# Eight instead of sixteen pairs of expert tiles in fixed order, four of them last; scatters at an even pace in the text; first gates, then places

## The chip, the core and the metric

The kernel runs on one core of a Trainium2 chip. The metric is the time of one execution on the device, in microseconds, the median of several runs. The engines are named as in the profile: PE is TensorE (matmuls), DVE VectorE, ACT ScalarE, POOL GpSimd, SP SyncE, which issues most of the transfers.

## The reference, cut to what matters

Two transformer blocks are computed for 256 tokens of width 1024. The change is in the last layer, a lookup among 16384 experts: every token picks 16 experts in each of eight heads, and only their values count.

```python
def _peer(h, w_q, subkeys, w_down, w_up):
    ...
        tv, tj = lax.top_k(cand, PEER_TOPK)
        eidx = jnp.take_along_axis(cidx, tj, axis=-1)
        w = jax.nn.softmax(tv, axis=-1)
        u = w_down[eidx]
        a = jax.nn.gelu(jnp.einsum('btd,btpkd->btpk', hblk, u).astype(jnp.float32))
        vv = w_up[eidx]
        return jnp.einsum('btpk,btpkd->btd', (w * a).astype(hblk.dtype), vv)
...
        x = x + ga2[:, None, :] * _peer(h, w_peer_q[l], peer_subkeys[l], peer_down[l], peer_up[l])
    return _rms_norm(x, g_norm_final)
```

## The kernel before

The kernel goes the other way round: it multiplies all tokens with all experts, and multiplies the result by a matrix of gates G that is zero where a token did not pick an expert. The 16384 experts are 128 tiles of 128, taken in 64 pairs, e = 0 to 63. The 256 tokens are two halves, tt = 0 and 1.

**Down.** `more_down` loads the down rows of one pair (`wr<-dn`), splits them into a high and a low part (`wh` on ScalarE, `wl` on VectorE), makes 48 matmuls of 256 columns and applies gelu; the result is a tile A in `store`. 28 of the 64 pairs are made while VectorE still works on routing and gates (`gen_chunk`, whose matmuls `acc<-L,R` count the tokens of each expert), 36 behind it. The gates go out to DRAM (`Gd`) and come back as `G`.

**Weigh.** `weigh(e)` multiplies A by G. For e < NS = 16 (static pairs) it does so in place. For the others the product goes to a tile `pt` (five buffers, shared with `Pc` below), which also gets the expert's number by an iota on GpSimd, and two indirect transfers from GpSimd scatter its rows to `Pd` in DRAM. The place of each row (`posi`) is such that experts used by the first half alone come first, then those used by both, by the second alone, and by none. The places follow from the counts by a chain of small operations on the tile `wk` and a few matmuls with `tri` and `oneb`.

**Up.** `static_up(e)` multiplies a static pair with its up rows: 4 blocks (2 tiles by 2 halves), a block being six matmuls of 512 columns. `row_up(i, used)` does so for a pair of scattered tiles: SyncE loads `Pc` from `Pd`, GpSimd gathers the up rows that belong to it (`wr<-up,Pc`, two tiles of 128 x 1024), ScalarE and VectorE split both into `ph`, `pl`, `wh`, `wl`. Which blocks a scattered tile j gets is fixed when the kernel is built: half 0 for j < T0, half 1 for T1 <= j < T2. That is right for the data if enough experts are used by the first half alone and not too many in all; `flag` says whether it is not, and in that case the blocks left out are made up for in the body of a `tc.If`:

```python
    for i, (n, op) in enumerate(((T1, ALU.is_lt), (T0, ALU.is_gt), (T2, ALU.is_gt))):
        dve.tensor_scalar(few[:, i:i + 1], few[:, i:i + 1], 128.0 * n, None, op0=op)
    ...
    with tc.If(v > 0, preferred_fallthrough_block=False):
        ...
        out_of = [(i, [[tt for tt in range(2) if tt not in blocks_of(2 * i + a)] for a in range(2)]) for i in range(NJ // 2)]
        ...
        for i, used in out_of:
            ph_, pl_, u_ = row_parts(i, used)
            ...
```

`few[0]` is the number of experts that the first half alone uses, `few[1]` of those that the first half uses, `few[2]` of those that any token uses; only the scattered tiles are counted. The body sums into banks of its own (`more`, in the trace `mt`), and at its end multiplies them by the layer's gate and adds them to x.

TensorE runs in the order of the text (class `Ordered`). On VectorE, ScalarE, GpSimd and SyncE the order is made by a scheduler when the kernel is built, and each engine then runs strictly in that order. Nearly all operations are recorded with one line, L342, so tiles are told apart by name. All multiplications are three products of high and low parts (`mm3`, `put_hl`).

Of the kernel before, what the change touches and what calls it, by code (L numbers as in the profile page):

```python
# [19 lines left out]

NEG = -1e30
TAIL = 8
NS = 16
NJ = 128 - 2 * NS
T0, T1, T2 = 61, 20, 83
ROOT2 = 4.0 ** 0.25
D = 1024
DFF = 2816
# [224 lines left out]
def build(tc, nc, I, out, dbg=None):  # L253
# [18 lines left out]
    def mt():  # L272
        return ps.tile([P, 512], F32, tag="mt", name=nm("mt"))
# [83 lines left out]
    def mm(o, l, r, start, stop):  # L357
        pe.matmul(o, l, r, start=start, stop=stop)
# [435 lines left out]
    with tc.tile_pool(name="a0", bufs=1) as hp:  # L794
# [14 lines left out]
        with tc.tile_pool(name="a0p", bufs=1) as pp0:  # L809
# [71 lines left out]
            for tt in range(2):  # L881
                b = acc()
# [580 lines left out]
    with tc.tile_pool(name="rp", bufs=1) as rp:  # L1463
# [116 lines left out]
        def gen_chunk(ch):  # L1580
            stg = rp.tile([P, P, 16], F32, tag="stg", name=nm("stg"), bufs=2)
            for q8 in range(2):
                t = (ch % 8) * 16 + q8 * 8
                L = L2[:, q8]
                R = rp.tile([P, 8, P], BF, tag="R", name=nm("R"), bufs=2)
                for i, o in ((0, L), (1, R)):
                    dve.tensor_tensor(o.rearrange("p t (n d) -> p t n d", d=4),
                                      iota1.rearrange("p (n d) -> p n d", d=4)[:, None].to_broadcast([P, 8, 32, 4]),
                                      slotb[:, i, t:t + 8][:, :, None, :].to_broadcast([P, 8, 32, 4]), op=ALU.is_equal)
                for q4 in range(2):  # L1590
                    q = slice(4 * q4, 4 * q4 + 4)
                    Lw = rp.tile([P, 4, 3, P], BF, tag="Lw", name=nm("Lw"), bufs=2)
                    dve.tensor_mul(Lw.rearrange("p t j (n d) -> p t j n d", d=4),
                                   L[:, q].rearrange("p t (n d) -> p t n d", d=4)[:, :, None].to_broadcast([P, 4, 3, 32, 4]),
                                   slotp[:, t + 4 * q4:t + 4 * q4 + 4][:, :, :, None, :].to_broadcast([P, 4, 3, 32, 4]))
                    m = mt()
                    for i in range(4):
                        for j in range(3):
                            mm(m[:, tsl(i)], R[:, 4 * q4 + i], Lw[:, i, j], start=j == 0, stop=j == 2)
                        n = t + 4 * q4 + i  # L1600
                        mm(cnt_b[0][:, ch // 8 * NJ:(ch // 8 + 1) * NJ], R[:, 4 * q4 + i], L[:, 4 * q4 + i, 2 * NS:],
                           start=n == 0, stop=n == 127)
                    o = 8 * q8 + 4 * q4
# [59 lines left out]
    M = wk[:, 0:192].bitcast(BF).rearrange("p (c j) -> p c j", c=4)
    totb = wk[:NJ, 192:448].bitcast(BF).rearrange("p (c t) -> p c t", c=4)
    pr = wk[:, 448:832]
    posi = wk[:, 832:928].bitcast(U32)
    u2 = wk[:, 928:1024].bitcast(BF).rearrange("p (b j) -> p b j", b=2)
    few = wk[:, 928:936]
    tri = mp_.tile([P, P], BF, tag="tri", name="tri", bufs=1)
    oneb = mp_.tile([P, P], BF, tag="oneb", name="oneb", bufs=1)  # L1670
    pool_.iota(wk[:, 832:833].bitcast(I32), pattern=[[0, 1]], base=0, channel_multiplier=1)
    act.copy(oneb, C("ones"))
    dve.tensor_copy(wk[:, 833:834], wk[:, 832:833].bitcast(I32))
    dve.tensor_scalar(tri, C("iota"), wk[:, 833:834], None, op0=ALU.is_gt)
    dve.tensor_scalar(wk[:, 928:1024].bitcast(BF), cnt_b[0][:, 0:2 * NJ], 0.5, None, op0=ALU.is_gt)
    dve.tensor_mul(M[:, 1], u2[:, 0], u2[:, 1])
    dve.tensor_sub(M[:, 0:3:2], u2, M[:, 1, None, :].to_broadcast([P, 2, NJ]))
    dve.tensor_sub(M[:, 3], oneb[:, :NJ], u2[:, 0])
# [1 line left out]
    b = mt()  # L1680
    for c in range(4):
        mm(b[:NJ, tsl(c)], M[:, c], oneb, start=c == 0, stop=c == 3)
    act.copy(wk[:NJ, 192:448].bitcast(BF), b[:NJ])
    more_down()
    b = mt()
    mm(b[:, :4 * NJ], tri, wk[:, 0:192].bitcast(BF), start=True, stop=False)
    for c in range(4):
        o = b[:, c * NJ:(c + 1) * NJ]
        mm(o, totb[:, c], tri[:NJ, :NJ], start=False, stop=False)
        for c_ in range(c):  # L1690
            mm(o, totb[:, c_], oneb[:NJ, :NJ], start=False, stop=False)
        mm(b[:, 4 * NJ + c:4 * NJ + c + 1], totb[:, c], oneb[:NJ, 0:1], start=False, stop=c == 3)
    dve.tensor_mul(pr, wk[:, 0:192].bitcast(BF), b[:, :4 * NJ])
    dve.tensor_add(pr[:, 0:2 * NJ], pr[:, 0:2 * NJ], pr[:, 2 * NJ:4 * NJ])
    dve.tensor_add(posi, pr[:, 0:NJ], pr[:, NJ:2 * NJ])

    dve.tensor_copy(few[:, 0:4], b[:, 4 * NJ:4 * NJ + 4])
    dve.tensor_add(few[:, 1:2], few[:, 1:2], few[:, 0:1])
    dve.tensor_add(few[:, 2:3], few[:, 2:3], few[:, 1:2])
    for i, (n, op) in enumerate(((T1, ALU.is_lt), (T0, ALU.is_gt), (T2, ALU.is_gt))):  # L1700
        dve.tensor_scalar(few[:, i:i + 1], few[:, i:i + 1], 128.0 * n, None, op0=op)
    dve.tensor_add(few[:, 0:1], few[:, 0:1], few[:, 1:2])
    flag = few[:, 4:5].bitcast(I32)
    dve.tensor_add(flag, few[:, 0:1], few[:, 2:3])
# [18 lines left out]
    def weigh(e):  # L1723

        G, A = gates(e), store[e]
        if e < NS:
            for a in range(2):
                for c in ((slice(0, 16),) if e >= 4 else (slice(0, 14), slice(14, 16))):
                    o = A[:, a * 256:(a + 1) * 256].rearrange("p (c t) -> p c t", c=16)[:, c]
                    dve.tensor_mul(o, o, Gl[:, :, (2 * e + a) % 8] if c.start else G[:, c, (2 * e + a) % 8])  # L1730
            return
        pt = mp_.tile([P, 2, W + 8], F32, tag="pt", name=nm("pt"), bufs=5)
        for a in range(2):
            i = 2 * e + a
# [175 lines left out]
```

## Time and profile before

| | |
|---|---|
| median of 3 runs | 1685.18 us (1684.71 to 1685.89) |
| profiled execution | 1687.74 us, its span 1685.9 us |
| TensorE busy | 1608.8 us, 95% of the span |
| VectorE, ScalarE, GpSimd busy | 1167.7 us (69%), 851.5 us (51%), 324.0 us (19%) |
| granted TensorE clock, mean | 0.981 |
| moved by DMA | 366.81 MB, 218 GB/s on the mean |

Times are from the start of the span. The span ends 13.8 us after TensorE's last matmul. A share of busy time is an average over stages: the last layer's stages are told apart by windows of the trace.

### The profile page before, as it was taken

To read this page: it belongs to the slowest core of one execution; us is meant where nothing else is said; L and a number is where in the kernel's file an instruction comes from. 1 tells how busy PE (TensorE), PEld (TensorE's weight loads), DVE (VectorE), ACT (ScalarE), POOL (GpSimd) and SP (SyncE) were. 2 spreads that over 40 slices of the span, in tenths; PEclk is the share of its full clock that TensorE was granted. 3 is DMA by queue.
4 is the path that set the end of the run, shared out by engine and by line. 5 is a ranking of instruction groups with operands and counts; after the bars stand their busy time and mean duration, and the time that the engine had idled before them with its cause. 6 is when DMAs were issued, how large, how long until landed. Compare 5 with 4: busy or idle time off the path is not lost. (4 is left out here: it accounts for less than half of the span.)

```text
span 1685.9 us, 28633 instructions
## 1 busy us (share of the span) xinstructions
PE 1608.8 (95%) x11241; PEld 1445.0 (86%) x11241; DVE 1167.7 (69%) x2110; ACT 851.5 (51%) x1307; POOL 324.0 (19%) x350
## 2 busy tenths in 40 slices
PE   7999999999999999988999999999789999999996
PEld 7878998879879998776778999999779999878885
DVE  6658875566678775666768989988566555476665
ACT  6654444356455444465545555545334444365564
POOL 0001000001010000110104600000573333554550
PEclk9999999999999999999999999999889999999998
DMA  7426876445348775455244456556899787598882
GB/s 291 174 74 224 315 277 217 160 165 189 116 156 322 277 275 175 156 192 202 100 133 160 171 176 225 202 200 227 270 311 319 247 277 244 187 344 285 287 287 101
DMA packets 106957, 366.81 MB, mean 218 GB/s; under 512 B 9120, under 2 KB 52896, under 8 KB 77888
## 3 DMA queue, kind: packets, MB, share of 16 engines
q1 hardware_dynamic: 89456, 307.82, 52.4%
q0 software_dynamic: 17072, 56.57, 9.3%
q8 instruction: 90, 1.47, 0.3%
q10 hardware_dynamic: 288, 0.52, 0.1%
q14 instruction: 51, 0.42, 0.1%
HBM read 334.01 MB, written 30.80 MB: 216 GB/s over the span
## 5 line engine op out<-in xcount | busy, mean ns | idle before, releaser
L342 DVE TENSOR_TENSOR wl<-wr,wh 128x1024 fp32r<-128x1024 f32 (+2 forms) x491 | 589.1, 1207 | 289.7 <-ACT wh L342 288.4
L342 ACT CAST wh<-wr 128x1024 fp32r<-128x1024 f32 (+2 forms) x511 | 526.7, 1034 | 491.8 <-PE acc L342 297.3
L342 PE MATMUL acc<-xh,wh 128*128 128x256 f32 x1472 | 421.0, 286 | 0.6 <-ACT xh L342 0.5
L342 PE MATMUL acc<-xl,wh 128*128 128x256 f32 x1472 | 413.4, 281 | 0.7 <-DVE xl L342 0.6
L342 PE MATMUL acc<-xh,wl 128*128 128x256 f32 x1472 | 412.7, 280 | 0.0
L342 PEld LDWEIGHTS acc<-xh,wh 128*128 128x128 f32 x1472 | 277.8, 189 | 2.5 <-issue 1.2
L342 PEld LDWEIGHTS acc<-xl,wh 128*128 128x128 f32 x1472 | 278.1, 189 | 1.3 <-DVE xl L342 1.3
L342 PEld LDWEIGHTS acc<-xh,wl 128*128 128x128 f32 x1472 | 277.6, 189 | 0.0
L342 PE MATMUL mt<-xh,wl 128*128 128x256 f32 x576 | 164.3, 285 | 12.7 <-DVE wl L342 12.7
L342 PE MATMUL mt<-xh,wh 128*128 128x256 f32 x576 | 163.7, 284 | 0.0
L342 PE MATMUL mt<-xl,wh 128*128 128x256 f32 x576 | 163.6, 284 | 0.0
L342 PE MATMUL acc<-wh,xh 128*128 128x512 f32 (+5 forms) x368 | 146.0, 397 | 15.9 <-ACT wh L342 7.6
L342 PE MATMUL acc<-wh,pl 128*128 128x512 f32 x376 | 149.8, 398 | 2.5 <-DVE pl L342 2.5
L342 PE MATMUL acc<-wh,ph 128*128 128x512 f32 x376 | 149.6, 398 | 1.9 <-ACT ph L342 1.3
L342 PE MATMUL acc<-wl,ph 128*128 128x512 f32 x376 | 149.5, 398 | 0.8 <-DVE wl L342 0.8
L342 PE MATMUL acc<-wl,xh 128*128 128x512 f32 (+5 forms) x368 | 142.4, 387 | 1.9 <-DVE wl L342 1.8
L342 PE MATMUL acc<-wh,xl 128*128 128x512 f32 (+5 forms) x368 | 142.4, 387 | 1.7 <-DVE xl L342 1.7
L342 POOL TENSOR_TENSOR x<-x,row 128x256 f32<-128x256 f32 x16 | 23.5, 1468 | 566.1 <-ACT x L342 565.4
L1741 POOL DMA_INDIRECT Pd<-pt,wk x96 | 121.0, 1261 | 46.2 <-issue 17.7
L342 PEld LDWEIGHTS mt<-xh,wl 128*128 128x128 f32 x576 | 110.8, 192 | 13.4 <-DVE wl L342 13.4
L1787 POOL DMA_INDIRECT wr<-up,Pc x83 | 95.9, 1155 | 89.3 <-DVE wl L342 59.2
L342 PEld LDWEIGHTS mt<-xh,wh 128*128 128x128 f32 x576 | 110.8, 192 | 0.4
(313 smaller groups left out, 2516.0 us busy)
## 6 DMA issues: line engine op xcount, KB each, us to landing
wr<-f SPq DMA_DIRECT2D x64, 1024.0 KB, 6.7
wr<-dn SPq DMA_DIRECT2D x64, 1024.0 KB, 5.2
wr<-ada SPq DMA_DIRECT2D x24, 1024.0 KB, 6.7
Gd<-stg SPq DMA_DIRECT2D x16, 1024.0 KB, 4.9
wr<-up SPq DMA_DIRECT2D x16, 1024.0 KB, 5.4
G<-Gd SPq DMA_DIRECT2D x15, 1024.0 KB, 9.0
wr<-m_g SPq DMA_DIRECT2D x10, 1024.0 KB, 5.0
row<-rows SPq DMA_DIRECT2D x16, 512.0 KB, 4.5
```

Source lines behind the costliest of these rows:

```text
L342: inst = f(*args, **kw)
L1741: nc.gpsimd.indirect_dma_start(Pv[j], bass.IndirectOffsetOnAxis(ap=posi[:, j:j + 1], axis=0), pt[:, a, 0:W], None)
L1787: nc.gpsimd.indirect_dma_start(r[:, a * 1024:(a + 1) * 1024], None, I["up"], bass.IndirectOffsetOnAxis(ap=Pc[:, a, 128:129].bitcast(U32), ...
```

## The change

NS = 16 becomes two numbers: static pairs are e < NA0 = 4 and e >= NB0 = 60, the 56 pairs between are scattered, so NJ goes from 96 to 112 tiles, and T0, T1, T2 from 61, 20, 83 to 70, 25, 95. The places and the flag are made after `weigh(0)` and the preparation of static pair 0 instead of ahead of them. Pairs 1 to 59 are weighed in their own order, in the text as many per down pair as come out even; `static_up` of 1, 2, 3 stands at every eighth down pair, that of 60 behind the last down pair, 61 and 62 among the gathered rows, and 63 at the end (before: nine between the down pairs, three behind them, three among the rows, one at the end). The views into `wk` move with the new widths.

```diff
-NS = 16
-NJ = 128 - 2 * NS
-T0, T1, T2 = 61, 20, 83
+NA0, NB0 = 4, 60
+NJ = 2 * (NB0 - NA0)
+T0, T1, T2 = 70, 25, 95
...
-                        mm(cnt_b[0][:, ch // 8 * NJ:(ch // 8 + 1) * NJ], R[:, 4 * q4 + i], L[:, 4 * q4 + i, 2 * NS:],
+                        mm(cnt_b[0][:, ch // 8 * NJ:(ch // 8 + 1) * NJ], R[:, 4 * q4 + i], L[:, 4 * q4 + i, 2 * NA0:2 * NB0],
...
-        if e < NS:
+        if not NA0 <= e < NB0:
...
-            j = 2 * (e - NS) + a
+            j = 2 * (e - NA0) + a
...
-    work = []
-    for g in (0, 4, 5, 6, 1, 7, 8, 2, 9, 3, 10, 11, 12, 13, 14, 15):
-        work.extend(range(4 * g, 4 * g + 4))
-
-    def weigh_some(n):
-        while work and n and work[0] < max(nxt[0] - 1, NS):
-            weigh(work.pop(0))
-            n -= 1
-
-    su = 0
-    weigh_some(5)
-    while nxt[0] < NE:
-        if (nxt[0] - 30) % 4 == 0:
-            static_up(su)
-            su += 1
-        more_down()
-        weigh_some(2)
-    nxt[0] += 1
-    weigh_some(len(work))
+    weigh(0)
+    part0 = static_parts(0)
+    b = mt()
+    mm(b[:, :4 * NJ], tri, Mf, start=True, stop=False)
...
+    static_up(0, *part0)
...
+    work = list(range(1, NB0))
+    steps = NB0 - nxt[0]
+    for k in range(NE - nxt[0]):
+        if k % 8 == 0 and 0 < k < 8 * NA0:
+            static_up(k // 8, *static_parts(k // 8))
+        more_down()
+        while work and (len(work) > (steps - 1 - k) * (NB0 - 1) // steps) and work[0] < nxt[0]:
+            weigh(work.pop(0))
+    for e in range(NB0, NE):
+        weigh(e)
+    static_up(NB0, *static_parts(NB0))
...
-    rest = list(range(su, NS - 1))
-    lead = 3
-    for _ in range(lead):
-        static_up(rest.pop(0))
+    rest = list(range(NB0 + 1, NE - 1))
     gap = len(seq) // (len(rest) + 1)
...
-    e = NS - 1
+    e = NE - 1
```

What the scheduler makes of it on VectorE, in the middle of the scatters. Before, the thirteenth scattered pair is `pt_13740`; the static pairs `A_9913` to `A_10121` are weighed in place ahead of it.

```order
L342 TENSOR_TENSOR wl_13351<-wr_13348,wh_13350 128x1024
L342 TENSOR_TENSOR A_9913<-A_9913,G_13606 128x256 x2
L342 TENSOR_TENSOR A_9988<-A_9988,G_13606 128x256 x2
L342 TENSOR_TENSOR A_10049<-A_10049,G_13606 128x256
L342 TENSOR_TENSOR wl_13355<-wr_13348,wh_13354 128x1024
L342 TENSOR_TENSOR A_10049<-A_10049,G_13606 128x256
L342 TENSOR_TENSOR A_10121<-A_10121,G_13606 128x256 x2
L342 TENSOR_TENSOR wl_13432<-wr_13429,wh_13431 128x1024
L342 TENSOR_TENSOR pt_13740<-A_12892,G_13738 128x2x128 x2
```

In the changed kernel the thirteenth to sixteenth scattered pairs (`pt_13692` to `pt_13873`) stand there, between the `wl` tiles of about the same down pairs.

```order
L342 TENSOR_TENSOR pt_13683<-A_11337,G_13538 128x2x128 x2
L342 TENSOR_TENSOR wl_13325<-wr_13318,wh_13324 128x1024
L342 TENSOR_TENSOR wl_13398<-wr_13395,wh_13397 128x1024
L342 TENSOR_TENSOR pt_13692<-A_11410,G_13690 128x2x128 x2
L342 TENSOR_TENSOR pt_13798<-Arow,G_13690 128x2x128 x2
L342 TENSOR_TENSOR wl_13402<-wr_13395,wh_13401 128x1024
L342 TENSOR_TENSOR pt_13805<-Arow,G_13690 128x2x128 x2
L342 TENSOR_TENSOR pt_13873<-A_11639,G_13690 128x2x128 x2
L342 TENSOR_TENSOR wl_13473<-wr_13470,wh_13472 128x1024
```

All products there are scattered ones, and none is in place. Further on, at the place where a scattered pair comes only once in a down pair (the thirteenth behind the gates has `wl_13892` and `wl_13896`), the changed kernel has made 34 of them:

```order
L342 TENSOR_TENSOR pt_14528<-A_13557,G_14526 128x2x128 x2
L342 TENSOR_TENSOR wl_13819<-wr_13812,wh_13818 128x1024
L342 TENSOR_TENSOR pt_14596<-A_13632,G_14526 128x2x128 x2
L342 TENSOR_TENSOR wl_13892<-wr_13889,wh_13891 128x1024
L342 TENSOR_TENSOR wl_13896<-wr_13889,wh_13895 128x1024
L342 TENSOR_TENSOR pt_14603<-A_13747,G_14526 128x2x128 x2
```

Before, the corresponding place comes after 18 scattered pairs, the last of them `pt_13998`:

```order
L342 TENSOR_TENSOR pt_13998<-A_13358,G_13928 128x2x128 x2
L342 TENSOR_TENSOR wl_13541<-wr_13538,wh_13540 128x1024
L342 TENSOR_TENSOR pl_14085<-A_9842,ph_14084 128x512
L342 TENSOR_TENSOR wl_13545<-wr_13538,wh_13544 128x1024
L342 TENSOR_TENSOR A_10269<-A_10269,G_14080 128x256 x2
```

So sixteen more scattered pairs stand ahead of that `wl`. The last place is the branch. On VectorE of the changed kernel the last sums of the static pairs (`x<-acc,ga`) stand ahead of the load of the flag, and behind the branch the body begins with two `pl` and then `wl`; in before the same kinds of instructions stand there.

```order
L342 TENSOR_TENSOR x_18613<-acc_13027,ga 128x512
L1843 TENSOR_LOAD wk
L1847 COMPARE_AND_BRANCH
L1847 UNCONDITIONAL_BRANCH
L342 TENSOR_TENSOR pl_17527<-Pc_17521,ph_17526 128x2x128
L342 TENSOR_TENSOR pl_17556<-Pc_17550,ph_17555 128x2x128
L342 TENSOR_TENSOR wl_17531<-wr_17523,wh_17530 128x1024
L342 TENSOR_TENSOR wl_17535<-wr_17523,wh_17534 128x1024
```

The body's own length moves with the numbers T0, T1, T2 and NJ: TensorE has 504 matmuls in it, where it had 408.

## Rows read from the trace of the kernel before

**Rows 1.** Windows: start:end, length, busy us (instructions) by engine, clock, DMA share, GB/s.

```profile
1000.00:1100.00 100.00, 99.98 (x1093) 98.39 (x1091) 91.65 (x179) 52.13 (x71) 0.00 (x0) 1.00 0.59 212
1180.00:1260.00 80.00, 63.38 (x436) 59.45 (x436) 47.86 (x100) 27.05 (x34) 51.60 (x76) 0.87 0.86 285
1260.00:1300.00 40.00, 40.00 (x310) 38.66 (x310) 24.63 (x36) 18.57 (x22) 14.58 (x20) 1.00 0.97 342
1480.00:1660.00 180.00, 180.00 (x773) 144.89 (x772) 122.16 (x127) 106.36 (x127) 86.91 (x75) 1.00 0.84 290
```

**Rows 2.** Timeline of TensorE: start, busy us, operation, [idle before <-releaser].

```profile
1221.52 0.58 PE L342 MATMUL mt<-xh,wl 128*128 128x256 f32 x1 [5.78 <-DVE wl L342]
...
1250.78 0.58 PE L342 MATMUL mt<-xh,wl 128*128 128x256 f32 x1 [5.97 <-DVE wl L342]
...
1474.77 0.50 PE L342 MATMUL acc<-wh,ph 128*128 128x512 f32 x1 [0.56 <-ACT wh L342]
```

**Rows 3.** Timeline of VectorE in the scatter stage.

```profile
1206.08 1.59 DVE L342 TENSOR_TENSOR pt<-Ax,G 128x256 f32<-128x256 f32 x4 [4.55 <-DMA Pd<-pt,wk]
...
1218.89 0.76 DVE L342 TENSOR_TENSOR pt<-A,G 128x256 f32<-128x256 f32 x2 [7.01 <-DMA Pd<-pt,wk]
...
1248.79 0.80 DVE L342 TENSOR_TENSOR pt<-A,G 128x256 f32<-128x256 f32 x2 [6.81 <-DMA Pd<-pt,wk]
```

**Rows 4.** Timeline of GpSimd, the first scatters.

```profile
1193.62 4.89 POOL L1741 DMA_INDIRECT Pd<-pt,wk  x1 [11.40 <-DVE wk L342]
...
1202.01 0.97 POOL L1741 DMA_INDIRECT Pd<-pt,wk  x1 [0.30 <-issue]
```

**Rows 5.** Timeline of TensorE, between down pairs and static blocks.

```profile
1298.42 0.39 PE L342 MATMUL acc<-wh,ph 128*128 128x512 f32 x1
...
1304.02 0.28 PE L342 MATMUL mt<-xh,wh 128*128 128x256 f32 x1
...
1332.38 0.28 PE L342 MATMUL mt<-xh,wh 128*128 128x256 f32 x1
```

**Rows 6.** Groups of TensorE: operation xcount | busy us, mean ns | idle before.

```profile
L342 PE MATMUL acc<-wh,ph 128*128 128x512 f32 x376 | 149.6, 398 | 1.9 <-ACT ph L342 1.3 <-ACT wh L342 0.6
...
L342 PE MATMUL mt<-Lw,R 128*128 128x128 bf16 x768 | 63.5, 223 | 5.5 <-DVE Lw L342 5.4
L342 PE MATMUL acc<-L,R 128*128 128x96 bf16 x256 | 53.3, 208 | 0.0
```

**Rows 7.** Timeline of TensorE, its last matmul.

```profile
1671.67 0.40 PE L342 MATMUL acc<-wh,pl 128*128 128x512 f32 x1
```

**Rows 8.** GpSimd's last gathers, the gathers' landing times, and sizes by issue.

```profile
1646.15 1.17 POOL L1787 DMA_INDIRECT wr<-up,Pc  x1 [0.31 <-issue]
1647.62 0.93 POOL L1787 DMA_INDIRECT wr<-up,Pc  x1 [0.30 <-issue]
...
DMA to landing us min/median/max: 4.4/5.8/8.8
...
Pc<-Pd SPq DMA_DIRECT2D x20, 136.0 KB, 4.1
```

**Rows 9.** Timeline of VectorE, the last gathered rows and the end.

```profile
1652.21 1.22 DVE L342 TENSOR_TENSOR wl<-wr,wh 128x1024 fp32r<-128x1024 f32 x1
1653.35 0.42 DVE L342 TENSOR_TENSOR pl<-Pc,ph 128x256 fp32r<-128x256 f32 x1
1653.68 1.22 DVE L342 TENSOR_TENSOR wl<-wr,wh 128x1024 fp32r<-128x1024 f32 x1
...
1665.93 0.68 DVE L342 TENSOR_TENSOR pl<-A,ph 128x512 fp32r<-128x512 f32 x1
...
1670.70 0.69 DVE L342 TENSOR_TENSOR x<-acc,ga 128x512 f32<-128x512 f32 x1 [0.71 <-PE acc L342]
1674.44 1.89 DVE L342 TENSOR_TENSOR x<-x,x 128x512 f32<-128x512 f32 x3 [3.06 <-issue]
1676.26 0.68 DVE L342 TENSOR_TENSOR x<-acc,ga 128x512 f32<-128x512 f32 x1
```

**Rows 10.** Timeline of ScalarE, a cast of up rows.

```profile
1663.70 1.05 ACT L342 CAST wh<-wr 128x1024 fp32r<-128x1024 f32 x1 [1.75 <-PE acc L342]
```

More of the change, by code (lines that the diff above doesn't have):

```diff
@@ L1662, in build @@
     wk = xp.tile([P, 1024], F32, tag="row", name="wk", bufs=2)
[L1663 to L1668, printed above, removed]
+    Mf, uf = wk[:, 0:2 * NJ].bitcast(BF), wk[:, 784:784 + NJ].bitcast(BF)
+    M = Mf.rearrange("p (c j) -> p c j", c=4)
+    totf = wk[:NJ, 224:480].bitcast(BF)
+    totb = totf.rearrange("p (c t) -> p c t", c=4)
+    pr = wk[:, 224:224 + 4 * NJ]
+    posi = wk[:, 672:672 + NJ].bitcast(U32)
+    u2 = uf.rearrange("p (b j) -> p b j", b=2)
+    few = wk[:, 896:904]
+    pid = wk[:, 904:906]
     tri = mp_.tile([P, P], BF, tag="tri", name="tri", bufs=1)
     oneb = mp_.tile([P, P], BF, tag="oneb", name="oneb", bufs=1)
-    pool_.iota(wk[:, 832:833].bitcast(I32), pattern=[[0, 1]], base=0, channel_multiplier=1)
+    pool_.iota(pid[:, 0:1].bitcast(I32), pattern=[[0, 1]], base=0, channel_multiplier=1)
     act.copy(oneb, C("ones"))
-    dve.tensor_copy(wk[:, 833:834], wk[:, 832:833].bitcast(I32))
-    dve.tensor_scalar(tri, C("iota"), wk[:, 833:834], None, op0=ALU.is_gt)
-    dve.tensor_scalar(wk[:, 928:1024].bitcast(BF), cnt_b[0][:, 0:2 * NJ], 0.5, None, op0=ALU.is_gt)
+    dve.tensor_copy(pid[:, 1:2], pid[:, 0:1].bitcast(I32))
+    dve.tensor_scalar(tri, C("iota"), pid[:, 1:2], None, op0=ALU.is_gt)
+    dve.tensor_scalar(uf, cnt_b[0][:, 0:2 * NJ], 0.5, None, op0=ALU.is_gt)
     dve.tensor_mul(M[:, 1], u2[:, 0], u2[:, 1])
@@ L1682, in build @@
         mm(b[:NJ, tsl(c)], M[:, c], oneb, start=c == 0, stop=c == 3)
-    act.copy(wk[:NJ, 192:448].bitcast(BF), b[:NJ])
+    act.copy(totf, b[:NJ])
     more_down()
[L1685 to L1704, printed above, removed]
     upb = [[acc(), acc()], [acc(), acc()]]
@@ L1767, in static_parts, with static_up @@
         return ph, pl, parts(r)
-    def static_up(e):
-        ph, pl, u = static_parts(e)
+    def static_up(e, ph, pl, u):
         for a in range(2):
@@ L1800, in row_up @@
                     up(upb, ph, pl, u, a, tt, half, False, False)
-    work = []
-    for g in (0, 4, 5, 6, 1, 7, 8, 2, 9, 3, 10, 11, 12, 13, 14, 15):
-        work.extend(range(4 * g, 4 * g + 4))
-    def weigh_some(n):
-        while work and n and work[0] < max(nxt[0] - 1, NS):
-            weigh(work.pop(0))
-            n -= 1
-    su = 0
-    weigh_some(5)
-    while nxt[0] < NE:
-        if (nxt[0] - 30) % 4 == 0:
-            static_up(su)
-            su += 1
-        more_down()
-        weigh_some(2)
-    nxt[0] += 1
-    weigh_some(len(work))
+    weigh(0)
+    part0 = static_parts(0)
+    b = mt()
+    mm(b[:, :4 * NJ], tri, Mf, start=True, stop=False)
+    for c in range(4):
+        o = b[:, c * NJ:(c + 1) * NJ]
+        mm(o, totb[:, c], tri[:NJ, :NJ], start=False, stop=False)
+        for c_ in range(c):
+            mm(o, totb[:, c_], oneb[:NJ, :NJ], start=False, stop=False)
+        mm(b[:, 4 * NJ + c:4 * NJ + c + 1], totb[:, c], oneb[:NJ, 0:1], start=False, stop=c == 3)
+    dve.tensor_mul(pr, Mf, b[:, :4 * NJ])
+    dve.tensor_add(pr[:, 0:2 * NJ], pr[:, 0:2 * NJ], pr[:, 2 * NJ:4 * NJ])
+    dve.tensor_add(posi, pr[:, 0:NJ], pr[:, NJ:2 * NJ])
+    dve.tensor_copy(few[:, 0:4], b[:, 4 * NJ:4 * NJ + 4])
+    dve.tensor_add(few[:, 1:2], few[:, 1:2], few[:, 0:1])
+    dve.tensor_add(few[:, 2:3], few[:, 2:3], few[:, 1:2])
+    for i, (n, op) in enumerate(((T1, ALU.is_lt), (T0, ALU.is_gt), (T2, ALU.is_gt))):
+        dve.tensor_scalar(few[:, i:i + 1], few[:, i:i + 1], 128.0 * n, None, op0=op)
+    dve.tensor_add(few[:, 0:1], few[:, 0:1], few[:, 1:2])
+    flag = few[:, 4:5].bitcast(I32)
+    dve.tensor_add(flag, few[:, 0:1], few[:, 2:3])
+    static_up(0, *part0)
     def blocks_of(j):
         return [tt for tt, t in ((0, j < T0), (1, T1 <= j < T2)) if t]
+    work = list(range(1, NB0))
[9 more added lines that the diff above has]
+    static_up(NB0, *static_parts(NB0))
     order_ = [(i, (blocks_of(2 * i), blocks_of(2 * i + 1))) for i in range(NJ // 2)]
@@ L1842, in build @@
         if rest and n % gap == gap - 1:
-            static_up(rest.pop(0))
-    while rest:
-        static_up(rest.pop(0))
-    e = NS - 1
+            static_up(rest[0], *static_parts(rest.pop(0)))
+    e = NE - 1
     ph, pl, u = static_parts(e)
```

## The prediction

> **What bounds the kernel now.** I read the windows first. TensorE has work in 99.98 of 100 us where the gates are made, in all of 180 us where the gathered rows are multiplied, and in 63.38 of 80 us between 1180 and 1260 us, where the scatters begin [rows 1]. That one stage has slack. In the list of TensorE's waits it is two of 5.78 and 5.97 us, both for VectorE's `wl` [rows 2]; in VectorE's list the same time is a wait for a landed scatter: the product `pt` of a pair needs one of five buffers, and stands in front of `wl` in VectorE's order [rows 3]. On GpSimd a scatter is issued in 0.97 us when nothing disturbs it, the first one took 4.89 us [rows 4]. Before 1180 us the change leaves all as it is but for the width of one kind of matmul.
>
> **The straight path.** The multiplications by up rows come in blocks of six matmuls of 512 columns. 24 of them, a `static_up`, lie between 1298.42 and 1304.02 us, and from there to 1332.38 four down pairs and one more `static_up` [rows 5]: a block is 1.40 us, a `static_up` 5.60, a down pair (28.36 − 5.60) / 4 = 5.69. The blocks of before: x376 of each of three products [rows 6] are 1128 matmuls, 188 blocks. Its code has 64 static and 124 gathered blocks outside `tc.If`, so the body of `tc.If` was not run. After the change there are 32 static and 70 + 70 = 140 gathered ones, 172, which takes 16 x 1.40 = 22.4 us off TensorE.
>
> That is not given back in full, because the end follows from when the scatter stage lets go. Buffers are recycled at a pace that rows 3 show: the sixth pair's product begins at 1206.08, the tenth's at 1218.89, the eighteenth's at 1248.79, so 3.20, 3.74, or over all 3.56 us a pair. The text of the changed code spreads the pairs, but VectorE's built order does not: 34 pairs stand before the `wl` of the thirteenth down pair, where 18 stood before. I take 3.56 (over the longest stretch). The 34th product then begins at 1206.1 + 28 x 3.56 = 1305.8. Added: 1.0 for counting matmuls of 112 instead of 96 columns (between 0 and 1.9: 128 columns take 223 ns, 96 take 208 [rows 6], half of the difference, 7.5 ns, times 256); 0.7 for a `pl` of 0.68 us [rows 9] that now stands ahead of the places on VectorE; 2.0 for the last product (0.80 [rows 3]) and the `wl` behind it (1.22 [rows 9]). At 1309.5 TensorE gets the thirteenth down pair, and behind it lie 24 x 5.69 = 136.6, six `static_up`, 33.6, and 140 x 1.40 = 196.0; the stretch from the last matmul (1671.67 + 0.40 = 1672.07 [rows 7]) to the span's end at 1685.9 stays, 13.8, and 0.6 for the start of the gathers (0.56 before the first [rows 2]). Sum 1690.1: **+4.2 us** on the span. Bounds: 3.20 a pair gives −5.9, 4.0 (if twice the length loads the queue more than before) +16.5; the start of the static blocks earlier, and `weigh` of 60 to 63 in place (eight products), lie in the stretch behind the scatters, where VectorE was busy 24.63 of 40 us [rows 1], and cost nothing there.
>
> **The branch.** The step that decides is another one. The flag is a sum of three comparisons, and is above zero if fewer than 128 x T1 experts are used by the first 128 tokens alone, or more than 128 x T0 by them at all, or more than 128 x T2 by any. I counted with the reference's own inputs and routing. For the experts of pairs 16 to 63 (before) these are 2718, 7584 and 10359 against 2560, 7808 and 10624: flag 0, as the 188 blocks say. For pairs 4 to 59 they are 3185, 8751 and 12015 against 3200, 8960 and 12160. 3185 is less than 3200, by 15: **the flag is 1, and the body of `tc.If` runs**.
>
> The body does what the fixed choice of blocks left out, 224 − 140 = 84 blocks in 34 pairs: 24 pairs of two blocks, one of one, one of three, then eight of four. By TensorE alone that is 84 x 1.40 = 117.6 us. By transfers: the first 26 pairs fetch two tiles of 512 KB each and a `Pc` of 136 KB [rows 8], 1.19 MB for 2.80 us of matmuls; together 30.4 MB. The best rate that a window shows is 342 GB/s, at a DMA share of 0.97 [rows 1]: 3.47 us a pair. So these pairs wait for DMA, the last eight, 5.60 us each, don't.
>
> Where it starts: SyncE and GpSimd reach the branch early (GpSimd's last gather was issued by 1648.55 [rows 8], 23.5 us before TensorE's end), so four pairs, as many as `wr` has buffers, are fetched by then. VectorE comes late: it has products of the static blocks ahead of the branch, and its first instruction behind it began 3.06 us after its last one ended, at 1674.44 [rows 9], 2.37 us after TensorE. Then two `pl` (0.33 apart) and a `wl`, 1.22: 1676.3. TensorE gets one matmul in, 0.23. In terms of before's clock:
> - TensorE-bound: 1676.1 + 117.6 = 1793.7, or 121.6 behind 1672.07.
> - DMA-bound: the first `wr` is free at 1677.5 (second `wl`); 30.4 − 4 x 1.19 = 25.7 MB are left, 75.1 us at 342 GB/s; from a gather's issue to its landing at least 4.4 us [rows 8], of which 1.5 are transfer, so 2.9 more: 1755.5. Cast 1.05 [rows 10], `wl` 1.22 and two blocks 2.80 bring the 26 pairs to 1760.6; 8 x 5.60 more: 1805.4, or 133.3.
>
> At the end four VectorE instructions hang on the last sums instead of one, and a jump follows again: 0.68 + 2 x 0.63 + 3.06 = 5.0 where 2.37 stood [rows 9], +2.7. I take the DMA-bound sum: **+136.0**; TensorE-bound it is +124.3. If the rate were that of the row stage, 290 GB/s at a share of 0.84 [rows 1], 13.5 more; that window was not full, so I stay near 342. If neither jump costs anything, 6.1 less.
>
> In all +4.2 + 136.0 = +140.2. The profiled execution took 1687.74 us with a span of 1685.9; the median of the runs is 1685.18, and the difference is added to that: **1825.4 us**.
>
> [...]
>
> [...]
>
> **The rivals.**
> - *The body is bound by TensorE (and VectorE).* VectorE needs 0.33 + 2 x 1.14 = 2.6 us for a pair of two blocks and GpSimd two gathers, 0.93 to 1.17 and 0.30 between [rows 8], 2.5: both below 2.80. For it: such pairs stood between four-block ones in the row stage and never stopped TensorE, 180 of 180. Against it: those averaged 4.2 us a pair. Time 1685.18 + 4.2 + 124.3 = 1813.7.
> - *The body is not run.* The margin is 15 experts in 3200. If the chip's own rounding or other drawn inputs turn it, the straight path is all: 1685.18 + 4.2 = 1689.4, between 1679.3 (3.20 us a pair) and 1701.7 (4.0).
> - *Faster than before*, the other side: the body is not run and the scatters recycle at less than 3.41 us a pair (there 28 x 0.15 us give back 4.2); at 3.20 it is 1679.3. If the pace of the text held and no pair stood in a `wl`'s way, up to 40 us less; VectorE's order speaks against it.
>
> **How the numbers follow.** Body run and DMA-bound 0.50, body run and TensorE-bound 0.34, not run 0.16. The likeliest gives 1825.4. Its bounds and those of the second case: 1813.7 with the fast pace, −10, is 1804; 1825.4 with the slow pace, +12, or the low rate, +13.5, is 1838, both together 1851. The range 1804 to 1848 holds nearly all of 0.84 and leaves the case without the body out. A measurement tells 0.2%, 3.4 us, from no change. Within the case not run: faster below 3.29 us a pair, 0.35; slower above 3.53, 0.45. So faster 0.055, same 0.03, slower 0.915.
>
> **What would show it.** In the profile after: matmuls `mt<-wh,ph` of 512 columns, 168 for each of three products, behind the last `static_up`, and their absence if the body is not run. The 172 blocks otherwise: 344 in each group of `acc<-wh,ph`. A first wait of some 4 us on TensorE at the body's start, DMA share above 0.9 in its first 90 us, waits of about 0.7 us a pair for `wh` or `wl` that GpSimd's gathers end; TensorE full in its last 45. In the scatter stage VectorE's waits for `Pd` reach to about 1305 us. What would make it wrong: the count on the chip on the other side of 3200, or gathers that move more or less than 342 GB/s in a stretch where nothing else moves.

## The result

The changed kernel takes 1869.0 us (median of 4 runs, 1864.4 to 1873.5) where before takes 1685.54 in the same comparison: a ratio of 1.108, 95% interval 1.105 to 1.112. Some executions of the kernel before run slower, at 1711 to 1739 us and a granted clock of 0.970 to 0.978 (0.979 to 0.986 in the others), and are left out of every comparison here. Forecast were 1825.4 us in a range of 1804 to 1848. It is slower, and the mechanism that was forecast, the body of `tc.If` that now runs, is most of it; but it is slower by more than forecast, +183.5 us on the median, +178.9 between the profiled spans (1864.8 against 1685.9).

The profile after splits that difference into three pieces: the straight path (all that runs outside the body), the body, and the end. The first view is the groups of TensorE's matmuls (columns as in [rows 6]):

```profile
L342 PE MATMUL acc<-wh,ph 128*128 128x512 f32 x344 | 135.5, 394 | 1.2 <-ACT ph L342 1.2
...
L342 PE MATMUL mt<-wh,ph 128*128 128x512 f32 x168 | 67.1, 399 | 1.5 <-ACT wh L342 1.5
```

344 and 168 are the numbers forecast: 172 blocks outside the body, 84 in it. The timeline of TensorE after gives the times that matter (start of the thirteenth down pair, start of the first block behind the last down pair, last matmul of the last static block, first and last matmul of the body):

```profile
1307.22 0.28 PE L342 MATMUL mt<-xh,wh 128*128 128x256 f32 x1
...
1499.91 0.39 PE L342 MATMUL acc<-wh,ph 128*128 128x512 f32 x1
...
1718.07 0.40 PE L342 MATMUL acc<-wh,pl 128*128 128x512 f32 x1
1719.72 0.50 PE L342 MATMUL mt<-wh,ph 128*128 128x512 f32 x1 [1.25 <-ACT wh L342]
...
1850.10 0.39 PE L342 MATMUL mt<-wh,pl 128*128 128x512 f32 x1
```

- The straight path ends at 1718.07 + 0.40 = 1718.47, where before ended at 1672.07 [rows 7]: **+46.4**, forecast +4.2.
- The body ends at 1850.49: **+132.0**, forecast 133.3 to this point.
- From there to the end of the span are 14.3 us where 13.8 stood: **+0.5**, forecast +2.7.

Their sum is 178.9. So one piece is wrong, the straight path, and inside it one stretch: the thirteenth down pair starts at 1307.2 (forecast 1309.5), the 156 blocks behind the down pairs take 218.56 us (forecast 218.4), but between them the down pairs end at 1499.9 where the forecast's own terms (1309.5 + 136.6 + 2 x 5.60) give 1457.3. The list of TensorE's waits after, from 1195 to 1500 us, says what for (us in total, times, longest; "issue" is time in which the engine waited for nothing that the profile shows):

```profile
PE mt L342 <- DVE wl L342: 45.5, 14, 6.6
PE mt L342 <- ACT wh L342: 9.8, 1, 9.8
PE acc L342 <- DVE wl L342: 6.3, 2, 3.4
PE mt L342 <- issue: 2.7, 1, 2.7
```

In before the same list, from 1195 to 1460 us, has one line:

```profile
PE mt L342 <- DVE wl L342: 12.7, 3, 6.0
```

The waits of after don't stop where the bunch of scatters ends: 31.6 us of them lie behind 1307 us. In that stretch TensorE is also slower while it works, busy for 160.99 us where the forecast's terms (136.6 + 11.2) are 147.8, at a mean granted clock of 0.92, where it is 1.00 in the static and gathered blocks behind it, from 1500 to 1680 us (columns as in [rows 1]):

```profile
1307.20:1499.90 192.70, 160.99 (x1202) 155.67 (x1201) 81.00 (x107) 67.26 (x78) 78.13 (x100) 0.92 0.60 204
```

The cause of the waits shows at 1335 us, where only one scattered pair comes per down pair. GpSimd's timeline after:

```profile
1335.49 0.21 POOL L342 IOTA pt<- 128x8 int32 x2 [4.69 <-DMA Pd<-pt,wk]
1336.24 2.00 POOL L1723 DMA_INDIRECT Pd<-pt,wk  x1 [0.54 <-DVE pt L342]
1338.55 0.96 POOL L1723 DMA_INDIRECT Pd<-pt,wk  x1 [0.30 <-issue]
1345.20 0.21 POOL L342 IOTA pt<- 128x8 int32 x2 [5.69 <-DMA Pd<-pt,wk]
1345.95 0.98 POOL L1723 DMA_INDIRECT Pd<-pt,wk  x1 [0.53 <-DVE pt L342]
...
1474.83 2.00 POOL L1723 DMA_INDIRECT Pd<-pt,wk  x1 [0.53 <-DVE pt L342]
```

VectorE's timeline after, its products there:

```profile
1335.49 0.76 DVE L342 TENSOR_TENSOR pt<-A,G 128x256 f32<-128x256 f32 x2 [2.67 <-DMA Pd<-pt,wk]
...
1345.29 0.76 DVE L342 TENSOR_TENSOR pt<-A,G 128x256 f32<-128x256 f32 x2 [6.77 <-DMA Pd<-pt,wk]
```

The iota that writes an expert's number into `pt` stands on GpSimd right behind the scatters of the pair whose buffer it takes over, five pairs back. So GpSimd issues two scatters, waits 5.69 us for these very scatters to land, writes the number of the pair five on, and only then may issue the next pair, whose product has long been there. That is a ring: scatter, landing, iota, scatter, with one pair in it at a time. From the scatters at 1336.24 to those at 1474.83, sixteen pairs later, it takes 8.66 us a pair, where TensorE asks for one in 5.69. VectorE, ahead by its five buffers, waits for the same landing, and its `wl` behind that. The longest wait, 9.8 us for `wh` at the last down pairs, comes of the same delay: on ScalarE that `wh` stands behind a cast of the first `Pc`, which waits until the scatters are through; the run with the numbers late below has no such wait:

```profile
1494.62 0.58 PE L342 MATMUL mt<-xh,wh 128*128 128x256 f32 x1 [9.79 <-ACT wh L342]
```

```profile
1493.01 0.62 ACT L342 CAST ph<-Pc 128x512 fp32r<-128x512 f32 x1 [14.51 <-DMA Pc<-Pd]
```

GpSimd's built order in the changed kernel, near there (`pt_14823` takes over the buffer of `pt_14603`, `pt_14832` that of `pt_14671`):

```order
L1723 DMA Pd<-pt_14603,wk 14336x264 x2
L342 IOTA pt_14823 128x8 x2
L1723 DMA Pd<-pt_14671,wk 14336x264 x2
L342 IOTA pt_14832 128x8 x2
L1723 DMA Pd<-pt_14680,wk 14336x264 x2
```

Each iota waits for the landing of the scatters in the row above it, which have just been issued. Before had the same order and the same ring. Its GpSimd timeline has the waits, up to 5.97 us, in rows that the prediction did not use:

```profile
1270.90 0.98 POOL L1741 DMA_INDIRECT Pd<-pt,wk  x1 [0.54 <-POOL pt L342]
...
1355.82 0.21 POOL L342 IOTA pt<- 128x8 int32 x2 [5.97 <-DMA Pd<-pt,wk]
1356.57 1.84 POOL L1741 DMA_INDIRECT Pd<-pt,wk  x1 [0.53 <-POOL pt L342]
1358.71 0.96 POOL L1741 DMA_INDIRECT Pd<-pt,wk  x1 [0.30 <-issue]
1363.64 0.21 POOL L342 IOTA pt<- 128x8 int32 x2 [3.98 <-DMA Pd<-pt,wk]
...
1439.40 1.28 POOL L1741 DMA_INDIRECT Pd<-pt,wk  x1 [0.53 <-POOL pt L342]
```

It was hidden because a static block stood behind every fourth down pair: four pairs had 28.36 us [rows 5], 7.09 each, and the ring took about 7.3 (scatters at 1270.90 and 1439.40, 23 pairs apart). Why a round takes 8.66 us in the one kernel and 7.3 in the other no run shows; in these stretches the median wait of an iota for the landing is 4.8 us against 4.0, and the median scatter takes 1.94 us against 0.98.

### The profile page after: what moved, and what is told of

The parts are those of the page before. It is cut to its first block, busy times and chain, and to the rows that moved or that the text cites. A ratio compares the mean times of both kernels' runs of the same rounds, so it can differ in the third digit from the quotient of the medians.

```text
span 1864.8 us, 30157 instructions
## 1 busy us (share of the span) xinstructions
PE 1732.0 (93%) x11649; PEld 1536.8 (82%) x11649; DVE 1258.5 (67%) x2213; ACT 927.1 (50%) x1402; POOL 445.6 (24%) x461
## 3 DMA queue, kind: packets, MB, share of 16 engines
q0 software_dynamic: 29216, 100.16, 14.7%
## 5 line engine op out<-in xcount | busy, mean ns | idle before, releaser
L342 ACT CAST wh<-wr 128x1024 fp32r<-128x1024 f32 (+3 forms) x574 | 592.1, 1035 | 573.5 <-PE acc L342 311.2
L342 DVE TENSOR_TENSOR wl<-wr,wh 128x1024 fp32r<-128x1024 f32 (+3 forms) x554 | 662.8, 1208 | 247.6 <-ACT wh L342 241.6
L1768 POOL DMA_INDIRECT wr<-up,Pc x162 | 202.6, 1251 | 131.6 <-DVE wl L342 65.5
L342 PE MATMUL mt<-xh,wl 128*128 128x256 f32 x576 | 173.1, 300 | 48.2 <-DVE wl L342 45.5
L342 PEld LDWEIGHTS mt<-xh,wl 128*128 128x128 f32 x576 | 118.6, 206 | 51.5 <-DVE wl L342 48.6
L1723 POOL DMA_INDIRECT Pd<-pt,wk x112 | 133.8, 1195 | 52.4 <-DVE pt L342 25.1
L342 PE MATMUL acc<-wl,ph 128*128 128x512 f32 x344 | 136.5, 397 | 6.3 <-DVE wl L342 6.3
L342 PE MATMUL acc<-wh,pl 128*128 128x512 f32 x344 | 137.9, 401 | 0.7 <-DVE pl L342 0.7
L342 PE MATMUL acc<-wh,ph 128*128 128x512 f32 x344 | 135.5, 394 | 1.2 <-ACT ph L342 1.2
L342 DVE TENSOR_TENSOR pt<-A,G 128x256 f32<-128x256 f32 x100 | 37.9, 423 | 135.7 <-DMA Pd<-pt,wk 115.2
```

The costliest lines, as they stand in the source:

```text
L342: inst = f(*args, **kw)
L1768: nc.gpsimd.indirect_dma_start(r[:, a * 1024:(a + 1) * 1024], None, I["up"], bass.IndirectOffsetOnAxis(ap=Pc[:, a, 128:129].bitcast(U32), ...
```

## The experiments

After the result my theory was the ring: GpSimd's order sets 8 to 9 us a pair, and the body is a separate cost. Against it stood three others: the straight path is as predicted and the body costs the rest; full DMA engines or too few buffers make the waits; or the place of the pairs in VectorE's order makes them.

The kernel before took 1681 to 1694 us in these comparisons, so the kernels are compared with one another and by their own traces, and a difference of a few us between medians is not clear.

**The flag alone.** The limit T1 goes back below the count.

```diff
-T0, T1, T2 = 70, 25, 95
+T0, T1, T2 = 70, 24, 95
```

> The changed kernel with T1 = 24 instead of 25, nothing else: 3185 experts are not fewer than 24 x 128 = 3072, so the flag is 0. One scattered tile gets its second half in the fixed part, one block more. Theory (the body costs what the trace of after shows between the last acc matmul and the last mt matmul, 132.0 us, and 0.5 at the end): 1869.0 - 132.5 + 1.4 = 1737.9 us, still 52 above before, because the down pairs end about 43 us later than I had worked out. Rival (the straight path is what I predicted and the rest belongs to the body): 1689 to 1692 us.

1736.0 us (1719.9 to 1742.1), and no `mt<-wh,ph` is left among the groups. The body is a cost by itself, and the straight path alone is some 50 us slower than before. All kernels below have T1 = 24 unless said otherwise.

**The numbers late.** The iota is tied behind the last scatter issued, so that it comes just ahead of its own pair's scatters; by then the pair five back has four pairs' time to land.

```diff
-            pool_.iota(pt[:, a, 128:136].bitcast(I32), pattern=[[0, 8]], base=i * P, channel_multiplier=1)
+            num = pool_.iota(pt[:, a, 128:136].bitcast(I32), pattern=[[0, 8]], base=i * P, channel_multiplier=1)
+            after(num, sent[-1])
...
-            nc.gpsimd.indirect_dma_start(Pv[j], bass.IndirectOffsetOnAxis(ap=posi[:, j:j + 1], axis=0), pt[:, a, 0:W], None)
+            sent.append(nc.gpsimd.indirect_dma_start(Pv[j], bass.IndirectOffsetOnAxis(ap=posi[:, j:j + 1], axis=0), pt[:, a, 0:W], None))
```

> T1 = 24, and on GpSimd the iota of a pair is put behind the scatters of the pair ahead of it, instead of behind those of the fifth pair ahead, whose buffer it takes over. Theory (GpSimd's order makes a ring: scatter, landing, iota of the pair five on, next scatter, some 8.7 us a pair, where TensorE asks for one in 5.69): the ring opens, GpSimd issues a pair in about 3 us, the waits of the last 24 down pairs go and part of those of the first ten: 1660 to 1695 us. Rival (the landing of scatters is slow because the DMA engines are full, whatever GpSimd's order): within 8 us of the run with T1 = 24 alone.

1669.5 us (1665.1 to 1674.0), 66.5 less than with the flag alone, by the order of GpSimd's instructions: VectorE's order in the two traces is the same through the down pairs but for five swaps of neighbours. Its timeline at the place shown above of after: the iota waits for nothing, GpSimd waits for VectorE's products, 5.64 us apart, near the 5.69 that TensorE takes for a down pair [rows 5].

```profile
1339.66 0.98 POOL L1726 DMA_INDIRECT Pd<-pt,wk  x1 [2.81 <-DVE pt L342]
1340.95 1.28 POOL L1726 DMA_INDIRECT Pd<-pt,wk  x1 [0.31 <-issue]
1342.25 0.24 POOL L342 IOTA pt<- 128x8 int32 x2
1345.30 0.98 POOL L1726 DMA_INDIRECT Pd<-pt,wk  x1 [2.82 <-DVE pt L342]
```

All that is left of TensorE's waits in the down stage lies before 1283 us, 21.1 us. The ring is shown; slow landing as such is out. The list of waits from 1190 to 1440 us, and TensorE's last matmul:

```profile
PE mt L342 <- DVE wl L342: 21.1, 9, 5.3
```

```profile
1651.49 0.40 PE L342 MATMUL acc<-wh,pl 128*128 128x512 f32 x1
```

**Four buffers instead of five.**

```diff
-        pt = mp_.tile([P, 2, W + 8], F32, tag="pt", name=nm("pt"), bufs=5)
+        pt = mp_.tile([P, 2, W + 8], F32, tag="pt", name=nm("pt"), bufs=4)
...
-        Pc = mp_.tile([P, 2, W + 8], F32, tag="pt", name=nm("Pc"), bufs=5)
+        Pc = mp_.tile([P, 2, W + 8], F32, tag="pt", name=nm("Pc"), bufs=4)
```

> T1 = 24 and four pt buffers instead of five, nothing else. Theory (the ring closes over one pair at a time whatever the number of buffers, since the iota of the pair that takes over a buffer stands right behind its scatters): the later down pairs go at the same 8.7 to 9.3 us a pair, only the first ten lose some: 1730 to 1755 us. Rival (five buffers are too few for the landing time): 5/4 of the time between 1200 and 1500 us, 1790 us or more.

1740.0 us (1736.7 to 1746.8): 4 us more than with five, within the runs' spread. The ring has some 9 us here too (iotas at 1434.38 and 1443.44); more than five buffers were not tried:

```profile
1434.38 0.21 POOL L342 IOTA pt<- 128x8 int32 x2 [5.24 <-DMA Pd<-pt,wk]
1435.12 2.00 POOL L1723 DMA_INDIRECT Pd<-pt,wk  x1 [0.53 <-DVE pt L342]
1437.43 0.96 POOL L1723 DMA_INDIRECT Pd<-pt,wk  x1 [0.30 <-issue]
1443.44 0.22 POOL L342 IOTA pt<- 128x8 int32 x2 [5.05 <-DMA Pd<-pt,wk]
```

**The pace of the text, held on VectorE**, with GpSimd's order left, and then with the numbers late as well. `dve.on` makes VectorE's order that of the text.

```diff
+    dve.on = True
     work = list(range(1, NB0))
...
+    dve.on = False
     for e in range(NB0, NE):
         weigh(e)
```

> T1 = 24, and VectorE is held to the order of the text through the down pairs, so that two scattered pairs at most stand between the wl tiles of two down pairs, as the text says. GpSimd's order stays the scheduler's. Theory (GpSimd's ring, some 7 to 9 us a pair, against 5.69 / 1.74 = 3.3 us a pair that this pace asks for): VectorE waits for landed scatters at every step, and as its order is now strict TensorE waits too: not better than T1 = 24 alone, 1730 to 1800 us. Rival (VectorE's order, pairs bunched ahead of wl tiles, made the waits): they go, 1650 to 1690 us.

1750.7 us (1749.3 to 1755.2), 14.7 more than with the flag alone: an even pace by itself makes it worse. The waits for `wl` are 60.3 us ahead of down pairs and 17.5 ahead of static blocks, where the flag alone had 53.7 and 5.8: the ring is felt all through the stage.

> T1 = 24, the iota of a pair behind the scatters of the pair ahead of it on GpSimd, and VectorE held to the text's order through the down pairs. Theory (both causes apart: the ring made the later waits, the bunching the earlier ones, 21 us of waits that are left between 1218 and 1283 us with the numbers late): GpSimd needs 2.75 us a pair, the pace asks for one in 3.3: nearly no waits, 1645 to 1655 us. Rival (the earlier waits come from buffers and landing, not from where the pairs stand): 1660 to 1675 us, as with the numbers late alone.

1664.6 us (1663.1 to 1666.6), the lowest median of all, though its range overlaps that of the numbers late alone; 0.986 of before, 95% interval 0.983 to 0.989. The waits for `wl` shrink from 21.1 to 6.6 us, so the bunching did make them, and in that the theory holds. The time does not follow: the down pairs end at 1430.8 instead of 1431.9. The list has a new line, 5.6 us of "issue", TensorE is busy 6.9 us longer from 1195 us to the end of the down pairs (222.7 instead of 215.8), and from 1268 to 1272 us its granted clock was 0.60 and then 0.55; more on that at the end. The list from 1190 to 1432 us:

```profile
PE mt L342 <- DVE wl L342: 6.6, 2, 3.3
PE mt L342 <- issue: 5.6, 13, 0.8
```

The expectation of 1645 to 1655 was missed.

**All eight static pairs first**, with one static block after every fourth down pair, as before has it; GpSimd's order left.

```diff
-NA0, NB0 = 4, 60
+NA0, NB0 = 8, 64
...
-        if k % 8 == 0 and 0 < k < 8 * NA0:
-            static_up(k // 8, *static_parts(k // 8))
+        if k % 4 == 0 and 0 < k < 4 * (NA0 - 1):
+            static_up(k // 4, *static_parts(k // 4))
...
-    for e in range(NB0, NE):
-        weigh(e)
-    static_up(NB0, *static_parts(NB0))
```

> T1 = 24, all eight static pairs are the first eight (pairs 8 to 63 are scattered), and one static block follows every fourth down pair, six of them, the seventh pair's at the end. GpSimd's order is left as the scheduler makes it. Theory (GpSimd's ring of some 8.7 us a pair sets the end of the down stage): the stage ends where it ended, the static blocks that were behind it now lie in its waits, 4 x 5.60 less: about 1716 us. Rival (the ring is no limit by itself, a static block between four down pairs gives it the 7.1 us a pair that it had in before): the waits of the later down pairs go, 1690 to 1700 us.

1707.4 us (1704.5 to 1712.7), between the two. The rival was right on the down pairs: none waits after 1302 us, and they end at 1466. GpSimd lags behind instead (21 pairs from 1307.6 to 1457.5 us, 7.1 each), and with no static block left to cover it the first gathered block waits:

```profile
1486.04 0.79 PE L342 MATMUL acc<-wh,ph 128*128 128x512 f32 x1 [19.90 <-ACT wh L342]
```

So spacing hides the ring, as it did in before, and what it hides is paid where the cover ends.

**The same with the numbers late**, two static blocks kept behind the down pairs, and the same with VectorE's order held too.

```diff
-        if k % 4 == 0 and 0 < k < 4 * (NA0 - 1):
+        if k % 4 == 0 and 0 < k < 4 * (NA0 - 3):
...
+    for e in (NA0 - 3, NA0 - 2):
+        static_up(e, *static_parts(e))
     rest = []
```

> T1 = 24, eight static pairs first, one static block after every fourth down pair for pairs 1 to 4, those of 5 and 6 behind the last down pair, 7 at the end, and the iotas behind the scatters of the pair ahead. Theory (with the ring open the down stage is short of DMA and of VectorE's order, not of TensorE; two more static blocks in it cost little there, and two behind it cover the start of the gathers, 19.9 us of wait in the run with eight first): 1650 to 1665 us. Rival (moving static blocks gives nothing once the ring is open): 1667 to 1675 us.

1689.4 us (1681.4 to 1694.6): missed by both. The start of the gathers still waits 8.6 us, so the two static blocks did not cover it. 14.3 us of "issue" stand in TensorE's waits from 1232 to 1288 us, at a granted clock of 0.76.

> The same, and VectorE held to the order of the text through the down pairs. Theory: as with the pace held in the other arrangement, waits for wl go and the DMA engines are full through the down pairs; the static blocks among them ask for fewer bytes per us, so that less is lost to that: 1643 to 1657 us. Rival (full DMA engines bind the down stage wherever the static blocks stand): 1657 to 1668 us.

1669.4 us (1666.5 to 1670.5): not better than with four first and four last. Neither theory named the 8.8 us that the start of the gathers waits again here. So with the pace held the place of the static blocks made 5 us; without it, eight first was 20 us slower than four first and four last (1689.4 against 1669.5), with TensorE's stops by "issue" in its scatter stage, which the other kernel does not have. What the place as such is worth stays open.

**Before, with the numbers late.** The same edit as above on the kernel before.

> The kernel before, with the iota of a pair behind the scatters of the pair ahead of it on GpSimd. Theory (the ring holds in before too, 7.3 us a pair, and is hidden but for the stage between 1180 and 1260 us): that stage's waits of 5.8 and 6.0 us on TensorE shrink, the scatters after 1260 us end earlier, the gathers' start does not wait: 1670 to 1682 us. Rival (five buffers and the landing time set that stage, not the order): 1683 to 1688 us.

1681.7 us (1680.2 to 1686.3), just inside what was expected, but the two runs of before beside it took 1680.7 and 1689.8, so no gain is shown: the ring cost before little or nothing. TensorE's waits for `wl` are 12.4 us where 12.7 were, so the waits between 1180 and 1260 us are not the ring's; the run with pace and late numbers points to the bunching. In the same comparison the changed arrangement with the numbers late, 1669.5, is 12 us faster than this.

**The body in another order.** T1 = 25, so that the body runs; after every three short pairs one of four blocks.

```diff
+        full = [q for q in out_of if len(q[1][0]) + len(q[1][1]) == 4]
+        part = [q for q in out_of if len(q[1][0]) + len(q[1][1]) < 4]
+        out_of = [q for n in range(len(full)) for q in part[n * 3:n * 3 + 3] + full[n:n + 1]] + part[3 * len(full):]
```

> The changed kernel as it is (T1 = 25, the body runs), with the body's pairs in another order: after every three short pairs one of four blocks. Same work, same transfers. Theory (in the body's first 26 pairs TensorE waits for DMA, 85.8 us where its work is 72.8; over all 34 pairs 41 MB at the 369 GB/s seen there take 111 us, less than 117.6 of TensorE): the body, last acc matmul to last mt matmul, goes from 132.0 to 120 to 124 us. Rival (TensorE or VectorE bind the body): it stays at 130 to 134 us.

1856.5 us (1853.5 to 1862.1). The body takes 121.7 us, from 1715.73 to 1837.43, in place of 132.0. The windows of after, first 26 pairs and last eight, columns as in [rows 1]:

```profile
1719.70:1805.50 85.80, 80.95 (x312) 57.26 (x313) 71.67 (x78) 61.41 (x78) 62.39 (x50) 0.98 0.98 353
1805.50:1850.50 45.00, 44.99 (x193) 35.85 (x191) 24.62 (x26) 18.40 (x21) 13.80 (x10) 1.00 0.44 164
```

The window of the mixed body:

```profile
1716.90:1837.50 120.60, 119.62 (x504) 95.63 (x504) 95.95 (x103) 80.55 (x99) 70.68 (x60) 0.99 0.89 315
```

Same work and transfers, 10 us less: the short pairs did wait for DMA, at a share of 0.98, and the long ones left much of it idle, at 0.44.

**The body behind an open ring.** T1 = 25, numbers late.

> The changed kernel with T1 = 25, so that the body runs, and the iota of a pair behind the scatters of the pair ahead of it on GpSimd. Theory (body and ring are two separate costs that add up): the run with the numbers late, 1669.5, plus a body of 131 to 133 us, less one block of 1.4: 1798 to 1803 us. Rival (part of the body's price was a delay that the late scatters brought with them): below 1795 us.

1812.0 us (1807.8 to 1821.4). The body is 132.5 us again (1665.06 to 1797.53), so it adds up; the sum missed by 10 because the straight path ended at 1665.1, 13.2 us later than in the run with the numbers late. 14.8 us of "issue" stand in its scatter stage, of which the run with the numbers late has none.

## Why the prediction was wrong

- **The branch: right.** 3185 against 3200 decided it, by the kernel's own comparison; 504 matmuls in `mt` say that the body ran.
- **The body: right in mechanism and size.** 133.3 forecast to its last matmul, 132.0 measured. In its pieces: the start 1.25 instead of 4.0, the first 26 pairs 85.8 instead of 84.5 at 353 GB/s instead of 342, the last eight 45.0 instead of 44.8. The rival "bound by TensorE" is refuted by the mixed order.
- **The end of the body: too dear.** Forecast +2.7 (its own terms make 2.6), measured +0.5. VectorE's second jump was not there: in after its last sums follow one another without a gap.
- **The bunch of scatters: right in number, and in part by luck.** 3.56 us a pair put the 34th product at 1305.8, the thirteenth down pair at 1309.5; VectorE's row stands at 1305.43, TensorE's at 1307.22. But the pace was read off rows of a kernel with the same ring, and put down to buffers that come free; with the same buffers and GpSimd's order changed the products come 2.95 us a pair (the sixth pair's at 1200.40, the 34th's at 1283.12), and the thirteenth down pair starts at about 1284.
- **The step that failed** is the next one: "behind it lie 24 x 5.69 = 136.6". It takes a scattered pair per down pair as hidden, as it was in before, though before had a static block for every four and this kernel has one for eight. I had VectorE's order and the wait for a buffer, and did not ask what GpSimd's own order makes each scatter wait for. Its ring takes 8.66 us a pair, and TensorE lost 42.6 us by the end of the down pairs: 31.6 of waits and 13.2 of matmuls at a granted clock of 0.92, less the 2.3 by which it was early at the thirteenth. The sign that the prediction named shows it too: VectorE's waits for `Pd` were to reach to about 1305 us, and reach to 1474. The run with the numbers late, which moves the iotas, gives them back and more: its straight path ends at 1651.9, where the prediction's sum, with 1.4 for the one block more, is 1677.7. The other 25.8 are what the ring cost inside the bunch (1309.5 forecast for the thirteenth down pair, about 1284 in that run, from 1431.9 for the end of its down pairs less 136.6 and 11.2).
- **"The rival faster than before"** had the right direction for a reason that I had not seen: without the body, with the ring open and the pace held, the same arrangement takes 0.986 of before.

The 342 GB/s that I took for the ceiling was the best of the rows shown, not of the trace: before has 367 over the 20 us from 1225 to 1245, and after 388 over 20 us (1780 to 1800) and 374 over 40 (1785 to 1825), in its body. What makes the two jumps differ, 3.06 us around the body [rows 9] and 0.24 into it (below), no run here shows.

## What to carry to other kernels

When a pool's buffers go round over an engine that issues in order, look at what stands behind each transfer on that engine: here an operation that takes over the buffer of the transfer just issued made GpSimd wait for its landing (5.69 us at 1345 us), and it made no clear difference whether there were four buffers or five (1740.0 and 1736.0 us). Write down what covers a wait before the cover is moved: the ring that one static block for four down pairs hid in before made TensorE wait 31.6 us behind the bunch here, with one for eight. And where a kernel has a branch for data that do not fit, count the data against each limit whenever the limits or the range change.

## What the runs showed of the hardware

Two things. In the changed kernel VectorE's instruction behind the branch into the body began 0.24 us after the last one ahead of it, where the first one behind the jump around the body began 3.06 us after it in before [rows 9]:

```profile
1717.11 0.69 DVE L342 TENSOR_TENSOR x<-acc,ga 128x512 f32<-128x512 f32 x1 [0.71 <-issue]
1718.05 0.42 DVE L342 TENSOR_TENSOR pl<-Pc,ph 128x256 fp32r<-128x256 f32 x1 [0.24 <-issue]
```

The other is that TensorE stops without a wait. In the fastest kernel (numbers late, pace held) matmuls that start 0.12 us apart suddenly start up to 1.11 apart, with "issue" as the only reason that the profile shows:

```profile
1265.66 0.28 PE L342 MATMUL mt<-xh,wl 128*128 128x256 f32 x1
1266.62 0.28 PE L342 MATMUL mt<-xh,wh 128*128 128x256 f32 x1 [0.67 <-issue]
1266.73 0.30 PE L342 MATMUL mt<-xl,wh 128*128 128x256 f32 x1
1266.87 0.28 PE L342 MATMUL mt<-xh,wl 128*128 128x256 f32 x1
1266.98 0.28 PE L342 MATMUL mt<-xh,wh 128*128 128x256 f32 x1
1268.09 0.37 PE L342 MATMUL mt<-xl,wh 128*128 128x256 f32 x1 [0.83 <-issue]
```

The windows around it show a DMA share of 1.16 just before, and TensorE's granted clock fall from 1.00 to 0.60 and 0.55 behind a stretch in which it was busy for 0.65 of 2 us:

```profile
1258.00:1260.00 2.00, 2.00 (x19) 2.00 (x18) 0.00 (x0) 0.03 (x1) 1.68 (x3) 1.00 1.16 372
...
1266.00:1268.00 2.00, 0.65 (x4) 0.42 (x3) 1.22 (x1) 0.30 (x1) 1.51 (x3) 1.00 0.88 299
1268.00:1270.00 2.00, 1.76 (x6) 1.22 (x7) 0.00 (x0) 0.30 (x1) 1.00 (x3) 0.60 0.91 268
1270.00:1272.00 2.00, 2.00 (x12) 2.00 (x12) 1.23 (x2) 1.38 (x3) 0.00 (x0) 0.55 1.11 370
```

The stops took 5.6 us in that kernel, 5.1 in the one with eight first and pace held, and 14 to 15 in two others with an open ring, the last two in stretches with a DMA share of 0.87 and 0.89. A high DMA share alone does not bring them, though: with the numbers late alone TensorE works through 20 us at a share of 1.03 without one such stop.

```profile
1290.00:1310.00 20.00, 20.00 (x171) 20.00 (x170) 11.51 (x15) 9.35 (x11) 15.49 (x27) 1.00 1.03 387
```

These stops are part of what the three missed expectations above left out; what makes them stays open.
